# Order of the product blocks in seventeen of eighteen column-group pairs of a trunk kernel

## The chip, the cores and the metric

The kernel runs on one core of one Trainium2 chip. The metric is device time in microseconds, from the first to the last instruction of one execution; the median of the runs is compared. Lower is better.

## What is computed

The reference is a trunk of two layers on a sequence of 256 tokens with a model width of 2048: first a gated linear attention layer (GLA, 4 heads), then a retention layer (8 heads), each with an inner width of 4096, a silu gate, a norm in front and a residual add behind, and one last RMS norm.

```python
proj = h @ w_in                          # q, k, v, gate
q, k, v, gate = jnp.split(proj, ...)
...                                      # chunked attention with decay, per head
o = from_chunks(o)
o = o * lax.rsqrt(jnp.mean(o * o, axis=-1, keepdims=True) + EPS)   # GLA; retention: group norm
o = o.reshape(B, S, D_INNER) * head_g
return (o * jax.nn.silu(gate)) @ w_out
```

Nearly all of the arithmetic is in the products of the 256 tokens with the weights `w_in` and `w_out`.

## The kernel before

**Products.** Weights are read in groups of 512 columns; a group has 16 k-tiles of 128 rows. Float32 precision comes from three matmuls per k-tile and token tile: weights and activations are each split into a high part in a reduced format (hi) and the remainder (lo), and hi x xh, lo x xh and hi x xl are summed in PSUM (lines L360, L361 and L362 in pairs, L269 to L271 in single groups, L454 and L456 for q and k).

**Weights.** A raw chunk holds four k-tiles, 128 x 4 x 512, and is loaded by one DMA of 1 MB on SyncE's queue (L194) into one of four buffers (`raw`). A chunk is used as two units of two k-tiles. For each unit ScalarE writes hi (L220) and then VectorE lo = raw - hi (L221), two units ahead of TensorE, into three buffers each.

**Pairs.** Eighteen times, two groups of columns are computed together: a value group and a gate group of a head, or two groups of the output projection (then called first and second, too). For k-tiles 0 to 7 the two token tiles, two column groups and two halves of these k-tiles form a 2 x 2 by 2 x 2 block product, which is done with seven products (S1 to S7) where eight would be plain. Each S block is two units of six matmuls. K-tiles 8 to 15 are done plainly: V0 to V3 for the first group of columns and G0 to G3 for the second, one unit of twelve matmuls each. In the rows an `S4a` would be the first unit of S4, `S4b` the second.

**Combined weights.** Most of the seven products need sums of weight blocks. They are made in place in the raw chunk: when a unit of S1 has been split, GpSimd issues a DMA of 512 KB (L230) that adds another block of weights to it, and the result is what S5 needs; likewise S5 to S6, S6 to S4 (chunk x, of the first group) and S3 to S7 (chunk y, of the second). So S6 can be split only when the addend issued behind S5 has landed, S4 behind S6, S7 behind S3.

**Banks.** A pair has four result banks: "11" and "21" for the first column group (token tile 0 and 1), "12" and "22" for the second. S4 and V0 to V3 complete "21", S2 and V0 to V3 "11", S3 and G0 to G3 "12". The products S1, S6 and S7 go through one further bank (`psa`), S5 through another (`psb`), which becomes "22". When a bank is complete, VectorE adds it to its destination, the eviction: L737, L743 and L750 at the attention heads, L1023 at the output projection. The bank then goes to the next group.

**Order.** A tuple of block names per kind of pair is a hand-written order: `RET` for ten pairs next to attention heads (named g1p0, g2p0, g2p1, g3p0, and r0p, r1p, r2p, r4p, r5p, r6p for retention), `LATE` for two pairs of the output projection that open an output phase (ga0, gb0), `OUT` for five others (ga1, gb1, ra0, ra1, rb0), and `END` for the last pair (rb1). The same plan orders the loading of the chunks, the splits and the matmuls. ga0 and ga1, gb0 and gb1, ra0 and ra1, rb0 and rb1, and g2p0 and g2p1 follow each other without a group between them, which the text calls a join. Attention work, norms (L591 squares, L1027 multiplies by the norm's weights), rotary angles (L1216, L1217) and transposes run beside the products as side steps after each block. A scheduler places each engine's instructions, in the order given by priorities, so a side step may move by a few rows.

Of the kernel before, what the change touches and what calls it, by code (L numbers as in the profile page):

```python
# [57 lines left out]
def kernel(  # L58
# [60 lines left out]
        for j in range(raws_per_group):  # L119
            plan_units(plan_chunk(g, j))  # L120

    OUT = ("S1", "S2", "V0", "V1", "S5", "S3", "V2", "G0", "S6", "G1", "S7", "V3", "S4", "G2", "G3")
    RET = ("S1", "V0", "S2", "V1", "S5", "S3", "V2", "G0", "S6", "G1", "S7", "V3", "S4", "G2", "G3")

    LATE = ("S1", "S2", "V0", "V1", "S5", "S3", "G0", "G1", "S6", "V2", "S7", "V3", "S4", "G2", "G3")

    END = ("S1", "S2", "V0", "V1", "S5", "S3", "V2", "V3", "G0", "S6", "G1", "G2", "G3", "S7", "S4")

    def plan_pair(gp, gq, order):


        at = {}

        def chunk(key, g, j):
            if key not in at:
                at[key] = plan_chunk(g, j)
            return at[key]

        for block in order:
            kind, n = block[0], int(block[1])  # L140
            if kind in "VG":
                j, half = divmod(n, 2)
                c = chunk(kind + str(j), gp if kind == "V" else gq, 2 + j)
                units.append((c, half, half == 1, None))
            elif n == 2:
                plan_units(plan_chunk(gp, 1))
            else:
                c = chunk("y", gq, 1) if n in (3, 7) else chunk("x", gp, 0)
                plan_units(c, n in (4, 7), {1: (gq, 0), 5: (gq, 1), 6: (gp, 1), 3: (gq, 0)}.get(n))

    def plan_all():
        g = 0
        for part, (stage, heads) in enumerate((("gla", 2), ("gla", 2), ("ret", 4), ("ret", 4))):
            for h in range(heads * part, heads * part + heads):
                plan_group(g)
                if stage == "ret" and h % heads < heads - 1:
                    plan_pair(g + 1, g + 2, RET)
                    g += 3
                    continue
                if stage == "gla" and g > 0:  # L160
                    plan_pair(g + 1, g + 2, RET)
                    if h in TWICE:
                        plan_pair(g + 3, g + 4, RET)
                    else:
# [7 lines left out]
                g += rest + 1  # L172
            plan_pair(g, g + 1, LATE if stage == "gla" else OUT)
            plan_pair(g + 2, g + 3, END if g + 4 == n_groups else OUT)
            g += 4
# [726 lines left out]
    def gla_head(h):  # L902
# [37 lines left out]
        def gate_part():  # L940
            for t in range(2):
                silu(sgs[0], r, t)
                yield
# [32 lines left out]
        for gi in range(0 if h == 0 else 2 if h in TWICE else 1):  # L976
# [5 lines left out]
            if gi == 1:  # L982
                side.append(gate_part())
            pair_x(xhl, f"gp{g}_", "x0", pair_on(o, sg, v, r, r2, gi == 1, h in TWICE and gi == 0), RET, sparse=True)
            if cname:
# [45 lines left out]
    def out_half(first, final, name, later=None):  # L1031
# [13 lines left out]
        for pair in range(2):  # L1045
# [34 lines left out]

            order = END if last else LATE if pair == 0 and name[0] == "g" else OUT
            pair_x(ogt, f"{name}{pair}", name, on, order, drain_side, halves=last)
# [175 lines left out]
    def ret_head(h):  # L1258
# [86 lines left out]

        pair_x(xhl, f"rp{h}_", "x1", pair_on(o, sg, v, r, r2), RET)
        hw["sg"] = sg
# [124 lines left out]
```

## Time and profile before

| | |
|---|---|
| median of three runs | 1376.33 us (1376.2 to 1378.25) |
| profiled execution | 1376.41 us, of which the span is 1374.6 us |
| granted TensorE clock | 0.998 of full speed |
| TensorE matmul busy | 1359.6 us, 99% |
| TensorE weight load busy | 1133.4 us, 82% |
| VectorE busy | 1104.8 us, 80% |
| ScalarE busy | 832.0 us, 61% |
| GpSimd busy | 171.5 us, 12% |
| HBM read | 324.31 MB, mean 241 GB/s |

The profile covers one execution. Busy is the time in which an engine has an instruction running; matmuls overlap in the pipeline, so TensorE can be busy and still not at its full pitch. The span is shorter than the execution's time by what lies before the first and after the last instruction.

### The profile page before, as it was taken

The numbers are of one execution on the slowest core, as the hardware profiler recorded it, in microseconds if no ns is written. First come the engines' busy times: TensorE is split into PE (matmuls) and PEld (weight loads), VectorE is DVE, ScalarE is ACT, GpSimd is POOL, SyncE is SP. The second block draws the span as 40 slices with busy tenths as digits, with TensorE's granted clock in tenths as the row PEclk, the third lists the DMA queues.
The fourth block names the chain that finished last, engine by engine and source line by source line (L and its number), as shares of the span: only waits on it lengthen the run. The fifth ranks groups of instructions, "written<-read, shape, count | busy, mean of one in ns | idle before, by whom it ended". The sixth has DMA issues, their size and how long they took to land.

```text
span 1374.6 us, 17650 instructions
## 1 busy us (share of the span) xinstructions
PE 1359.6 (99%) x6500; PEld 1133.4 (82%) x6500; DVE 1104.8 (80%) x1517; ACT 832.0 (61%) x1060; POOL 171.5 (12%) x218
## 2 busy tenths in 40 slices
PE   8999999999999999999999999999999999999997
PEld 7888888888887888788888888888888888888876
DVE  6695896888897698887988888878768888887887
ACT  6676666655666766666655656446546465654665
POOL 1011110110122020111011111001201010100210
PEclk9999999999999999999999999999999999999999
DMA  9564785899899695699698969559989797964896
GB/s 359 212 245 161 208 252 188 208 273 317 233 267 275 179 266 197 189 262 281 184 296 262 292 204 291 180 191 254 266 341 236 251 236 252 241 246 165 226 299 170
DMA packets 58871, 331.76 MB, mean 241 GB/s; under 512 B 6928, under 2 KB 7440, under 8 KB 29856
## 3 DMA queue, kind: packets, MB, share of 16 engines
q1 hardware_dynamic: 34656, 238.96, 47.5%
q0 software_dynamic: 23408, 89.01, 32.7%
q10 hardware_dynamic: 720, 2.66, 0.5%
q8 instruction: 51, 0.84, 0.2%
q14 instruction: 36, 0.29, 0.1%
HBM read 324.31 MB, written 6.29 MB: 241 GB/s over the span
## 4 chain that ended last, share of the span: by engine, by line
PE 89%; DVE 4%; DMA 3%; ACT 2%; issue 1%; POOL 0%; ACTq 0%; DVEq 0%; POOLq 0%
PE rqk_ps L466 8%; PE rqk_ps L467 4%; PE rp__ps L361 4%; PE rp__ps L360 4%; PE rp__ps L362 4%; DMA raw<-in_w_all 3%; PE gqk_ps L466 2%; PE gv_ps L269 2%; PE gv_ps L270 2%; PE gv_ps L271 2%; DVE lo L221 2%; PE gg_ps L270 2%; PE gg_ps L269 2%; PE gp__ps L361 2%; PE gg_ps L271 2%; PE gp__ps L362 2%
## 5 line engine op out<-in xcount | busy, mean ns | idle before, releaser
L220 ACT ACTIVATE hi<-raw 128x1024 fp32r<-128x1024 f32 (+1 forms) x585 | 617.4, 1058 | 472.6 <-PE rqk_ps L466 69.0
L221 DVE TENSOR_TENSOR lo<-raw,hi 128x1024 fp32r<-128x1024 f32 (+1 forms) x585 | 710.4, 1223 | 228.2 <-ACT hi L220 221.2
L230 POOL DMA_DIRECT2D raw<-in_w_all x144 | 124.0, 861 | 653.7 <-DVE lo L221 450.9
L466 PE MATMUL rqk_ps<-xhl,hi 128*128 128x512 f32 x480 | 162.6, 397 | 0.0
L467 PE MATMUL rqk_ps<-xhl,lo 128*128 128x256 f32 x480 | 123.3, 281 | 0.0
L466 PEld LDWEIGHTS rqk_ps<-xhl,hi 128*128 128x128 f32 x480 | 88.1, 188 | 17.9
L467 PEld LDWEIGHTS rqk_ps<-xhl,lo 128*128 128x128 f32 x480 | 88.2, 189 | 3.6
L361 PE MATMUL rp__ps<-lo,xhl 128*128 128x512 f32 x192 | 74.9, 390 | 0.0
L362 PE MATMUL rp__ps<-hi,xhl 128*128 128x512 f32 x192 | 74.7, 389 | 0.0
L360 PE MATMUL rp__ps<-hi,xhl 128*128 128x512 f32 x192 | 69.8, 389 | 0.0
L361 PE MATMUL gp__ps<-lo,xhl 128*128 128x512 f32 x128 | 51.0, 399 | 0.8 <-DVE lo L221 0.8
L270 PE MATMUL gv_ps<-lo,xhl 128*128 128x512 f32 x128 | 50.9, 398 | 0.0
L270 PE MATMUL gg_ps<-lo,xhl 128*128 128x512 f32 x128 | 50.1, 392 | 0.0
L271 PE MATMUL gv_ps<-hi,xhl 128*128 128x512 f32 x128 | 50.0, 391 | 0.0
L362 PE MATMUL gp__ps<-hi,xhl 128*128 128x512 f32 x128 | 49.9, 390 | 0.0
L271 PE MATMUL gg_ps<-hi,xhl 128*128 128x512 f32 x128 | 49.9, 389 | 0.0
L466 PE MATMUL gqk_ps<-xhl,hi 128*128 128x512 f32 x144 | 49.4, 396 | 0.0
L360 PE MATMUL gp__ps<-hi,xhl 128*128 128x512 f32 x128 | 47.6, 393 | 0.3 <-ACT hi L220 0.3
L269 PE MATMUL gg_ps<-hi,xhl 128*128 128x512 f32 x128 | 46.7, 390 | 0.0
L269 PE MATMUL gv_ps<-hi,xhl 128*128 128x512 f32 x128 | 46.2, 393 | 0.0
L360 PEld LDWEIGHTS rp__ps<-hi,xhl 128*128 128x128 f32 x192 | 36.1, 188 | 7.5
L362 PEld LDWEIGHTS rp__ps<-hi,xhl 128*128 128x128 f32 x192 | 36.1, 188 | 7.5
(554 smaller groups left out, 2986.5 us busy)
## 6 DMA issues: line engine op xcount, KB each, us to landing
raw<-in_w_all SPq DMA_DIRECT2D x220, 1024.0 KB, 6.2
raw<-in_w_all POOLq DMA_DIRECT2D x144, 512.0 KB, 7.8
ogt<-xc POOLq DMA_DIRECT2D x2, 2048.0 KB, 11.8
resid<-in_x_n SPq DMA_DIRECT2D x2, 1024.0 KB, 13.0
xc<-ogt POOLq DMA_DIRECT2D x1, 2048.0 KB, 8.9
gg<-in_gn_g POOLq DMA_DIRECT2D x8, 256.0 KB, 4.0
gb<-in_gn_b POOLq DMA_DIRECT2D x8, 256.0 KB, 3.8
xc<-ogt ACTq DMA_DIRECT2D x1, 2048.0 KB, 7.5
```

What stands on the lines that cost most here:

```text
L220: a = nc.scalar.activation(hi[:, sl], src[:, sl], AF.Copy)
L221: b = nc.vector.tensor_tensor(lo[:, sl], src[:, sl], hi[:, sl].bitcast(F32), ALU.subtract)
L230: nc.gpsimd.dma_start(src, chunk_src(*then)[:, rows], accum_op=ALU.add)
L269: mm(ps, xh, hi[:, q, :], start=kt == 0, stop=False)
L270: mm(ps, xh, lo[:, q, :], start=False, stop=False)
L271: mm(ps, xl, hi[:, q, :], start=False, stop=kt == NKT - 1)
L360: mm(ps, xh, hi[:, q, :], start=start, stop=False, skip_group_check=True)
L361: mm(ps, xh, lo[:, q, :], start=False, stop=False, skip_group_check=True)
L362: mm(ps, xl, hi[:, q, :], start=False, stop=stop, skip_group_check=True)
L466: mm(ps[c], wh, rhs[:, kt, :, :], start=kt == 0, stop=False)
L467: mm(ps[c][:, 0, :], wl, rhs[:, kt, 0, :], start=False, stop=False)
```

## The change

The three tables `OUT`, `RET` and `LATE` change; `END` and all other code stay. S6 moves behind G1, that is behind both units that hold k-tiles 8 to 11 of the second group; S7 moves behind V3; S4 moves to the end of the pair.

```diff
--- before.py
+++ after.py
@@ -119,10 +119,10 @@
         for j in range(raws_per_group):
             plan_units(plan_chunk(g, j))
 
-    OUT = ("S1", "S2", "V0", "V1", "S5", "S3", "V2", "G0", "S6", "G1", "S7", "V3", "S4", "G2", "G3")
-    RET = ("S1", "V0", "S2", "V1", "S5", "S3", "V2", "G0", "S6", "G1", "S7", "V3", "S4", "G2", "G3")
-
-    LATE = ("S1", "S2", "V0", "V1", "S5", "S3", "G0", "G1", "S6", "V2", "S7", "V3", "S4", "G2", "G3")
+    OUT = ("S1", "S2", "V0", "V1", "S5", "S3", "V2", "G0", "G1", "S6", "V3", "S7", "G2", "G3", "S4")
+    RET = ("S1", "V0", "S2", "V1", "S5", "S3", "V2", "G0", "G1", "S6", "V3", "S7", "G2", "G3", "S4")
+
+    LATE = ("S1", "S2", "V0", "V1", "S5", "S3", "G0", "G1", "S6", "V2", "V3", "S7", "G2", "G3", "S4")
 
     END = ("S1", "S2", "V0", "V1", "S5", "S3", "V2", "V3", "G0", "S6", "G1", "G2", "G3", "S7", "S4")
```

The next rows are the order of instructions on an engine, without times. A number behind a name counts buffers; hi and lo are numbered by units through the whole program.

ScalarE at the end of the pair g2p1, before the change: hi177 is V3, hi178 and hi179 are S4, hi180 and hi181 G2 and G3; L713 is the silu of a gate, L734 and L495 belong to values.

```order
L220 ACTIVATE hi177_3714<-raw68_3490 128x1024
L220 ACTIVATE hi178_3724<-raw64_3248 128x1024
L734 ACTIVATE go5_3474<-gp5__psa_3477 128x512
L220 ACTIVATE hi179_3735<-raw64_3248 128x1024
L713 ACT_TABLE_LOAD
L713 ACTIVATE gsg4_3099<-gsg4_3099,rr_110 128x512
L220 ACTIVATE hi180_3759<-raw70_3610 128x1024
L495 ACTIVATE gv5_3476<-go5_3474,rr_110 128x512
L220 ACTIVATE hi181_3769<-raw70_3610 128x1024
```

The same place after the change: hi177 is the second unit of S7, hi178 and hi179 are G2 and G3, hi180 is the first unit of S4.

```order
L220 ACTIVATE hi177_3714<-raw67_3488 128x1024
L713 ACT_TABLE_LOAD
L713 ACTIVATE gsg4_3099<-gsg4_3099,rr_110 128x512
L220 ACTIVATE hi178_3738<-raw70_3610 128x1024
L495 ACTIVATE gv5_3486<-go5_3484,rr_110 128x512
L220 ACTIVATE hi179_3748<-raw70_3610 128x1024
L734 ACTIVATE go5_3484<-gp5__psa_3487 128x512
L220 ACTIVATE hi180_3759<-raw64_3248 128x1024
```

The load of the table and the silu stood between S4 and G2, and now stand between S7 and G2; the first split of S4 comes after both G blocks.

VectorE where ga1 ends and the q/k group g2qk begins, before: lo129 is G3, lo130 to lo132 are the first units of q/k; L1023 are evictions of the banks named ps21, ps12 and psb ("22").

```order
L221 TENSOR_TENSOR lo129_2849<-raw52_2691,hi129_2848 128x1024
L1023 TENSOR_TENSOR resid_104<-ga1_ps21_2616,resid_104 128x512
L1216 SCALAR_TENSOR_TENSOR ang_2583<-ang_2583 128x256
L221 TENSOR_TENSOR lo130_2862<-raw53_2703,hi130_2861 128x1024
L1217 TENSOR_SCALAR ang_2583<-ang_2583 128x256
L221 TENSOR_TENSOR lo131_2878<-raw53_2703,hi131_2877 128x1024
L1023 TENSOR_TENSOR resid_104<-ga1_ps12_2690,resid_104 128x512
L1023 TENSOR_TENSOR resid_104<-ga1_psb_2660,resid_104 128x512
L221 TENSOR_TENSOR lo132_2903<-raw54_2836,hi132_2902 128x1024
```

The same place after: lo128 and lo129 are S4, lo130 to lo132 again q/k.

```order
L221 TENSOR_TENSOR lo128_2839<-raw46_2421,hi128_2838 128x1024
L1217 TENSOR_SCALAR ang_2583<-ang_2583 128x256
L221 TENSOR_TENSOR lo129_2855<-raw46_2421,hi129_2854 128x1024
L1023 TENSOR_TENSOR resid_104<-ga1_ps12_2690,resid_104 128x512
L1023 TENSOR_TENSOR resid_104<-ga1_psb_2660,resid_104 128x512
L221 TENSOR_TENSOR lo130_2875<-raw53_2703,hi130_2874 128x1024
L221 TENSOR_TENSOR lo131_2885<-raw53_2703,hi131_2884 128x1024
L1023 TENSOR_TENSOR resid_104<-ga1_ps21_2616,resid_104 128x512
L221 TENSOR_TENSOR lo132_2903<-raw54_2814,hi132_2902 128x1024
```

The eviction of "21" stood ahead of the first q/k unit's lo and now stands behind the second unit's; those of "12" and "22" went the other way.

VectorE at the join of rb0 and rb1, before: lo565 is G3 of rb0, lo566 and lo567 are S1 of rb1, lo568 is the first unit of S2.

```order
L221 TENSOR_TENSOR lo565_11135<-raw214_10985,hi565_11134 128x1024
L1023 TENSOR_TENSOR resid_104<-rb0_ps21_10916,resid_104 128x512
L1027 TENSOR_TENSOR resid_104<-resid_104,fn0_10856 128x512
L221 TENSOR_TENSOR lo566_11152<-raw215_10997,hi566_11151 128x1024
L1027 TENSOR_TENSOR resid_104<-resid_104,fn0_10856 128x512
L221 TENSOR_TENSOR lo567_11169<-raw215_10997,hi567_11168 128x1024
L1023 TENSOR_TENSOR resid_104<-rb0_ps12_10984,resid_104 128x512
L1023 TENSOR_TENSOR resid_104<-rb0_psb_10958,resid_104 128x512
L221 TENSOR_TENSOR lo568_11201<-raw216_11122,hi568_11200 128x1024
```

After: lo565 is the second unit of S4 of rb0; lo566 to lo568 are the same units as above.

```order
L221 TENSOR_TENSOR lo565_11141<-raw208_10694,hi565_11140 128x1024
L1023 TENSOR_TENSOR resid_104<-rb0_ps12_10984,resid_104 128x512
L1023 TENSOR_TENSOR resid_104<-rb0_psb_10958,resid_104 128x512
L221 TENSOR_TENSOR lo566_11167<-raw215_10997,hi566_11166 128x1024
L1027 TENSOR_TENSOR resid_104<-resid_104,fn1_10858 128x512 x2
L1023 TENSOR_TENSOR resid_104<-rb0_ps21_10916,resid_104 128x512
L221 TENSOR_TENSOR lo567_11178<-raw215_10997,hi567_11177 128x1024
L221 TENSOR_TENSOR lo568_11201<-raw216_11100,hi568_11200 128x1024
```

Two L1027 and the eviction of "21" now stand between the two lo of S1, and nothing between the second of them and that of S2; before, one L1027 stood there, and two evictions behind it.

## Rows read from the trace of the kernel before

**Rows 1.** The page, part 1: busy us, share of the span, instructions.

```profile
PE 1359.6 (99%) x6500; PEld 1133.4 (82%) x6500; DVE 1104.8 (80%) x1517; ACT 832.0 (61%) x1060; POOL 171.5 (12%) x218
```

**Rows 2.** The chain that ended last, from 424 us: start, us, what.

```profile
425.05 10.03 DMA raw<-in_w_all
...
447.46 0.93 PE gqk_ps L454 x4
```

**Rows 3.** Busy time of each engine from 650 to 930 us.

```profile
650.00:930.00 280.00, 280.00 (x1389) 236.50 (x1387) 232.03 (x328) 158.73 (x194) 28.48 (x37) 1.00 0.78 239
```

**Rows 4.** Waits of TensorE in pairs: total us, times, longest.

```profile
PE gb_ps L361 <- DVE lo L221: 0.9, 3, 0.4
PE gp__ps L361 <- DVE lo L221: 0.8, 2, 0.5
PE ga_ps L361 <- DVE lo L221: 0.6, 2, 0.4
PE gp__ps L360 <- ACT hi L220: 0.3, 1, 0.3
...
PE rb_ps L361 <- DVE lo L221: 0.2, 1, 0.2
```

**Rows 5.** Timeline of TensorE, g2p1's end: start, us, what, [idle before].

```profile
437.53 0.50 PE L361 MATMUL gp__ps<-lo,xhl 128*128 128x512 f32 x1 [0.28 <-DVE lo L221]
437.87 0.39 PE L362 MATMUL gp__ps<-hi,xhl 128*128 128x512 f32 x1
...
439.26 0.50 PE L360 MATMUL gp__ps<-hi,xhl 128*128 128x512 f32 x1 [0.30 <-ACT hi L220]
...
440.52 0.51 PE L361 MATMUL gp__ps<-lo,xhl 128*128 128x512 f32 x1 [0.53 <-DVE lo L221]
```

**Rows 6.** The page, parts 5 and 6: groups of instructions, and DMA issues.

```profile
L221 DVE TENSOR_TENSOR lo<-raw,hi 128x1024 fp32r<-128x1024 f32 (+1 forms) x585 | 710.4, 1223 | 228.2 <-ACT hi L220 221.2
...
raw<-in_w_all POOLq DMA_DIRECT2D x144, 512.0 KB, 7.8
```

**Rows 7.** Timeline of ScalarE, the end of g2p1.

```profile
435.16 1.06 ACT L220 ACTIVATE hi<-raw 128x1024 fp32r<-128x1024 f32 x1 [2.25 <-DMA raw<-in_w_all]
436.24 1.28 ACT L713 ACT_TABLE_LOAD   x1
437.53 0.72 ACT L713 ACTIVATE gsg<-gsg,rr 128x512 f32<-128x512 f32 x1
```

**Rows 8.** Timelines of the weight loads and of VectorE, g2p1 to g3qk.

```profile
446.49 0.19 PEld L454 LDWEIGHTS gqk_ps<-xhl,hi 128*128 128x128 f32 x1 [0.42 <-DVE gsg L750]
...
445.75 0.68 DVE L750 TENSOR_TENSOR gsg<-gp__ps,gsg 128x512 f32<-128x512 f32 x1
```

**Rows 9.** Timelines of ScalarE and of TensorE at G2 of ga1.

```profile
326.52 2.01 ACT L220 ACTIVATE hi<-raw 128x1024 fp32r<-128x1024 f32 x2 [0.72 <-DMA raw<-in_w_all]
...
327.63 0.50 PE L360 MATMUL ga_ps<-hi,ogt 128*128 128x512 f32 x1 [0.25 <-ACT hi L220]
```

**Rows 10.** Timelines of VectorE, ScalarE and TensorE where rb0 meets rb1.

```profile
1326.93 0.68 DVE L1027 TENSOR_TENSOR resid<-resid,fn 128x512 f32<-128x512 f32 x1
1327.54 0.68 DVE L1061 TENSOR_TENSOR resid<-resid,rb_psa 128x512 f32<-128x512 f32 x1
...
1327.02 0.61 ACT L591 ACTIVATE sqj<-resid 128x512 f32<-128x512 f32 x1
...
1328.34 0.89 PE L360 MATMUL rb_ps<-hi,ogt 128*128 128x512 f32 x2
1329.40 0.50 PE L361 MATMUL rb_ps<-lo,ogt 128*128 128x512 f32 x1 [0.17 <-DVE lo L221]
...
1331.14 0.50 PE L361 MATMUL rb_ps<-lo,ogt 128*128 128x512 f32 x1
```

**Rows 11.** Timeline of VectorE behind the join of g2p0 and g2p1.

```profile
403.69 0.68 DVE L863 TENSOR_TENSOR w<-w,qk 128x256 f32<-128x256 f32 x1
...
407.24 0.28 DVE L861 TENSOR_TENSOR w<-lc 128x128 f32<-128x128 f32 x1
```

## The prediction, made before the changed kernel ran

> **What bounds the kernel now.** I read the page's busy times first: TensorE is busy for 1359.6 us, 99% of the span, VectorE for 80% and ScalarE for 61% [rows 1]. A full TensorE could still be slow inside, so I took its pitch next: four 512-column matmuls start within 0.93 us [rows 2], one per 0.23, and in the stretch from 650 to 930 us, which is retention pairs and q/k groups, it is busy for 280.00 of 280.00 [rows 3]. The change leaves every matmul in place, so it can only act on the moments at which TensorE waits. The view of waits lists them: in the pairs 0.9, 0.8, 0.6, 0.3 and 0.2 us of idle time [rows 4], and one of 0.25 at G2 of ga1 [rows 9]. A wait costs more than its idle time. A matmul shows 0.39 us although the next starts after 0.23, so 0.16 of the delay looks busy, and the first one after a wait shows 0.50, another 0.11 [rows 5]. I therefore price a wait at its idle time plus 0.27. With ten waits in all the pairs lose 3.1 + 2.7, about 6 us, some 0.4% of the span. Of these, the ones that open a pair behind a group stay as they are, since no block there moves.
>
> The reader should keep one cadence in mind. A unit of two k-tiles is split by ScalarE (hi, 1.06 [rows 7]) and then VectorE (lo, 1.22 [rows 6], or 1.14 from start to start when back to back, since the next one overlaps it by 0.08). TensorE works 12 x 0.227 = 2.72 on a V or G block and 6 x 0.227 = 1.36 on half of an S product. There are three hi and three lo buffers, so the hi of a unit can't start before TensorE has ended the unit three before it. A unit that stands behind two S units has 2.72 for 2.28 of splitting, and any further VectorE operation in front of its lo goes on TensorE's time.
>
> **What it removes.** (1) The fourth product's addend at the pair g2p1. The accumulating DMA issued at 425.05 took 10.03 us [rows 2]; ScalarE sat 2.25 for it, and a table load (1.28) and a silu (0.6 until the next starts) stood between this hi and that of G2 [rows 7]. TensorE waited 0.28 in S4b, then 0.30 and 0.53 in G2 [rows 5]: 1.11 + 3 x 0.27 = 1.9. After the change V3, S7, G2, G3 and S4a (12.2 us of TensorE) stand between S6b and S4b where G1, S7, V3 and S4a (9.5) stood, so the addend has 2.72 more than before, and it was only 0.28 + 0.16 late. The table load now stands ahead of the hi of G2. With t=0 at the end of V3, the hi of S7b ends by -1.6, the load by -0.3, the silu by 0.3, the hi of G2 by 1.4 and its lo by 2.6 to 2.8, against a first lo matmul at 2.72 + 2 x 0.227 = 3.17. So -1.9; its lower end is 0.9 left, if the lo comes 0.6 late.
>
> ScalarE's rows show the load ending at 437.52 and the silu starting at 437.53 [rows 7], with nothing between. The Trainium skill (ScalarE: Activation LUTs, section What ACT_TABLE_LOAD costs) gives the same 1.28 us for the load but adds a drain of 1.38 to every switch; the trace agrees with the first and shows no room for the second. By the page the lo of G2 would come at 4.2, and the sum below would be 1.0 + 0.3 higher here and 1.4 higher at the join of (5).
>
> (2) g2p1 to the next q/k group: its fourth bank waits 0.42 for L750, the eviction of "12" [rows 8], of which I count 0.27 as lost, since a weight load runs a little ahead of its matmul. "12" is now done a product earlier, and the bank that the fourth tile takes is that of "21", with six attention matmuls in front: -0.3. (3) G2 at ga1: its hi started on the raw chunk's landing [rows 9] and TensorE idled 0.25: 0.25 + 0.27 = -0.5. That chunk takes the buffer that G1's split frees, and G1 is now split right behind G0. Gains: 1.9 + 0.3 + 0.5 = **2.7**. In the nine other pairs of the RET order no wait of TensorE is released by a late split (the gp rows are g2p1's three, and there is no rp row [rows 4]), so more room for their addends is worth nothing.
>
> **What it adds.** S4 last means that the bank "21" is finished after "12" and "22", and that where two pairs meet six S units run on end (S4, S1, S2): each gives VectorE 1.36 us, and its lo takes 1.14. Three evictions (0.60 each from start to start, as L1027 [rows 10]) must fit in too.
>
> (4) ga1 to g2qk. The order shown has the eviction of "21" behind the lo of both first units of q/k. t=0 at the end of G3: eleven S4 matmuls remain (2.50), the fourth q/k matmul, which starts in that bank, is due at 2.50 + 3 x 0.227 = 3.17. The hi of g2qk/1 waits for S4a to leave its buffer (1.13) and ends at 2.25; its lo runs behind the previous one from 2.46 to 3.60; the eviction (0.68, as an L1027 or an L750 [rows 8, 10]) ends at 4.28. Late by 1.15 with the start-up, plus 0.11: **+1.25**. Bounds: 0, if the lo of g2qk/1 started before 1.3, and 1.7, if a hi is 0.4 later.
>
> (5) rb0 to rb1. t=0 as before; S4 ends at 2.72, S1a at 4.08. Before S1b's lo VectorE now has two evictions, the lo of S1a, two multiplications of L1027 and the eviction of "21". Evictions 0.06 to 1.3, lo S1a to 2.5; two L1027 (0.6 each from start to start [rows 10]) to 3.7, as the squares on ScalarE need only the two evictions (0.61 and an accumulator read, 0.72 each, to 2.5); eviction of "21" to 4.3; lo S1b to 5.5, where S1b's second matmul is due at 4.5: 1.0. The table load has moved between the hi of S1b and that of S2a, and V0, whose hi must wait for S1b and one more square, ends its lo at 10.5 against 9.7: 0.8. Three late points with 0.27 each give about 2.6, against 1.05 that this join loses today: L361 starts 1.06 behind the first of two L360 where two pitches, 0.45, would do (0.6), 0.11 behind it, and the same pattern of half the size in V0, whose L361 shows 0.50 [rows 10]. **+1.6**, bounds 0 (the join keeps its present loss) and +2.6.
>
> (6) g2p0 to g2p1. Between the lo of S4b and that of S1a VectorE now has two evictions (1.2), two products of w (0.68, so 0.6 from start to start) and four small ones (0.28, so 0.2) [rows 11]: from 0.3 on they last until 2.9, the lo of S1a until 4.1, and TensorE wants it at 3.2. **+1.1**, bounds 0 and 1.5. (7) gb0 to gb1: two squares, three evictions and transposes in the same six units; 1.05 against the present 0.4 + 0.27 [rows 4]: **+0.4**, bounds -0.65 and +1. (8) ga0 to ga1, ra0 to ra1 and the two v groups behind g1p0 and g3p0, where the last evictions stand just ahead of a lo with 0.0 to 0.3 in hand: together **+0.4**, bounds 0 and +2.
>
> Nothing else is priced: the number of DMAs, of splits and of evictions is the same, and SP's and GpSimd's issues move along with the units whose buffers they fill.
>
> **Sum**: -2.7 + 1.25 + 1.6 + 1.1 + 0.4 + 0.4 = **+2.0 us**. The profiled execution took 1376.41 us (1374.6 of span and 1.8 around it), and the median of the runs is 1376.33, so both give **1378.4**. A difference of 0.2% (2.75 us) is about the least that a measurement of this kernel can tell from no change.
>
> **Rivals.**
> *The joins hold (faster).* If VectorE enters each join a unit ahead, as it does today at most places, the evictions fit into that lead: then (4) to (8) cost 0 to 1 and 1373.6 to 1375 remains. For it: retention pairs run with no idle time at all at 80% VectorE [rows 1, 3]. Against it: the lead can be no more than the buffers allow, and my times above start from the earliest moment that they allow. The deciding point is the end of the lo of S1b at rb0|rb1, before or after 4.5 us behind G3. Chance 0.17; half of it passes -2.75.
>
> *The joins cost their upper bounds (slower).* One mechanism: VectorE has 8.2 us in six S units and a bill of 6 x 1.14 + 3 x 0.60 = 8.6, before any square, w or L1027; when its lead is gone before the run begins, each of these is paid in full. (4) 1.7, (5) 2.6, (6) 1.5, (7) 1.0 and (8) 2.0 are 8.8, less 2.7: +6, **1382.4**. For it: the DVE-released waits already outnumber the others [rows 4]. Against it: the long blocks G2 and G3 ahead of the run let VectorE catch up. It decides where the lo of S4b ends later than G3. Chance 0.25.
>
> *The addend was not the cause.* If S4's addend or G2's chunk lands as much later as it is wanted later, since the queues hold more at that moment (median 7.8 us today [rows 6]), the 2.4 of (1) and (3) stays and the additions come on top: +4.4, 1380.7. Against it: raw loads and addends keep their number and nearly their spacing. Chance 0.05.
>
> *A load of tables that blocks for longer.* If ScalarE is held for another 1.4 behind each of the two moved loads, G2 at g2p1 loses 1.3 of what (1) gives, and rb0|rb1 1.4 more: +4.7, 1381.1. The silu that follows a load within 0.01 us [rows 7] speaks against it. The Trainium skill (ScalarE: Activation LUTs, What ACT_TABLE_LOAD costs) is what would let one expect it. Chance 0.02.
>
> **How the numbers follow.** My sum has 0.51, with its own range from +0.3 to +3.3. Faster by more than 0.2%: half of the first rival, 0.08. Slower by more: 0.23 of the second rival, 0.06 of the last two and a tenth of the sum's own case, 0.05, which make 0.34. The rest, 0.58, is within 0.2%. The range that leaves out a tenth at each end runs from 1374.0, in the middle of the first rival, to 1382.0, just below the second's price.
>
> **What would show it.** Right: the three waits at g2p1 are gone and its ScalarE no longer waits for a DMA ahead of S4b; a wait of about 1 us in the L454 of the q/k group behind ga1, released by L1023; waits of L361 on lo at rb0|rb1 and g2p0|g2p1 of 0.5 to 1 us; no waits within the blocks of the retention pairs. Wrong: L454 starts at pitch there, or waits appear inside pairs at S6, V3 or S7, which I hold free.

## The result and the profile after

The changed kernel takes 1384.13 us (median of six runs, 1383.42 to 1387.11) against 1376.59 for the kernel before (six runs, 1376.2 to 1378.25). The ratio is 1.0056 with a 95% interval of 1.0046 to 1.0066, so it is slower by 6.3 to 9.1 us. The prediction was 1378.4 with a range up to 1382.0. The forecast was therefore wrong, by some 6 us and outside its range.

The page of the profiled execution after the change, its head and part 1 (answers to [rows 1]):

```profile
span 1381.6 us, 17654 instructions
...
PE 1361.2 (99%) x6500; PEld 1134.0 (82%) x6500; DVE 1106.9 (80%) x1517; ACT 831.3 (60%) x1060; POOL 173.0 (13%) x218
```

The span is 7.0 us longer, with the same 6500 matmuls, and TensorE's busy time grew by 1.6 only. The rest must be idle time, so the view of waits of TensorE comes next (total us, times, longest; answers to [rows 4]):

```profile
PE rqk_ps L466 <- DVE xhl L496: 2.4, 1, 2.4
...
PE rb_psa L361 <- DVE lo L221: 1.2, 1, 1.2
PE gqk_ps L454 <- DVE resid L1023: 1.0, 1, 1.0
PE gp__psa L361 <- DVE lo L221: 0.9, 1, 0.9
PE gb_ps L361 <- DVE lo L221: 0.8, 3, 0.4
...
PE gv_ps L270 <- DVE lo L221: 0.2, 1, 0.2
```

The first "..." stands for two waits of the opening, which are there before, too. Three of the first four rows shown are what the prediction named: the joins rb0|rb1 (term 5, `rb_psa`) and g2p0|g2p1 (term 6, `gp__psa`), and the fourth bank behind ga1 (term 4, `gqk_ps` released by the eviction L1023). The `gp__ps` rows of g2p1 are gone, as terms (1) and (3) wanted it. But the first row, the longest of all, is at a place that the prediction doesn't mention: the q/k group r0qk of the retention layer, which follows gb1.

The stretch that the prediction called full, 650 to 930 us (answer to [rows 3]; columns as there), starts with that wait. TensorE is busy for 2.41 us less than the 280.00 of before:

```profile
650.00:930.00 280.00, 277.59 (x1372) 234.46 (x1371) 230.81 (x323) 156.27 (x191) 27.79 (x36) 0.99 0.78 238
```

TensorE's timeline around it (start, us, instruction, [idle before]):

```profile
665.45 1.03 PE L694 MATMUL xt_tp<-ident,resid 128*128 128x128 f32 x8
668.89 0.79 PE L466 MATMUL rqk_ps<-xhl,hi 128*128 128x512 f32 x1 [2.41 <-DVE xhl L496]
...
669.70 0.63 PE L466 MATMUL rqk_ps<-xhl,hi 128*128 128x512 f32 x1
```

L694 transposes the residual (the layer's input) on TensorE, eight 128 x 128 blocks in a row; L496 on VectorE turns the transposed block into `xhl`, the hi and lo activations that L466 and L467 multiply. VectorE's timeline in the wait:

```profile
666.62 1.23 DVE L221 TENSOR_TENSOR lo<-raw,hi 128x1024 fp32r<-128x1024 f32 x1 [0.24 <-ACT hi L220]
667.76 0.68 DVE L307 TENSOR_TENSOR x_c<-x_f,x_c 128x512 f32<-128x512 f32 x1
668.36 0.48 DVE L496 SCALAR_TENSOR_TENSOR xhl<-xt_tp,smalls,xhl 128x256 fp32r<-128x256 f32 x1
```

The transposes are done at 666.5, but a lo (L221) and an addition of activation blocks (L307) stand ahead of L496 on VectorE, so the first `xhl` is ready at 668.84 and L466 starts at 668.89. VectorE isn't later here than before the change, when the same operations end at nearly the same times:

```profile
667.91 0.69 DVE L307 TENSOR_TENSOR x_c<-x_f,x_c 128x512 f32<-128x512 f32 x1
...
668.58 0.87 DVE L496 SCALAR_TENSOR_TENSOR xhl<-xt_tp,smalls,xhl 128x256 fp32r<-128x256 f32 x2
```

Before, TensorE goes on without a wait there: the `xhl` that VectorE writes at this time is one that is wanted later. The wait is 2.41, and it has a tail. Busy time in three stretches (us, then PE, PEld, DVE, ACT, POOL busy with counts, PEclk, DMA share, GB/s), after:

```profile
666.00:669.00 3.00, 0.59 (x6) 0.35 (x4) 2.76 (x7) 2.38 (x5) 0.00 (x0) 0.99 0.96 333
669.00:673.00 4.00, 4.00 (x14) 3.43 (x15) 3.49 (x13) 0.81 (x2) 0.00 (x0) 0.58 0.05 16
673.00:677.00 4.00, 4.00 (x25) 3.52 (x24) 2.36 (x2) 2.76 (x3) 0.00 (x0) 1.00 0.13 20
```

and the second of them before the change:

```profile
669.00:673.00 4.00, 4.00 (x24) 3.48 (x24) 4.00 (x8) 3.49 (x5) 0.00 (x0) 1.00 0.20 57
```

In the 4 us behind the wait the granted clock is 0.58, which means mostly the lower level of 1.2 GHz, and 14 matmuls fit in where 24 did: 10/24 x 4 = 1.7 us. Then it is 1.00 again. Wait and slow stretch make 4.1 us. In the prediction this place is free.

**Why these transposes.** The eviction of token tile 1 from a bank starts the transposes of its columns for the next layer. "21" of gb1 is column group 2, k-tiles 8 to 11 of the next layer; "22" is column group 3, k-tiles 12 to 15. Before, "21" was complete two blocks ahead of "22". TensorE's order there before (no times; `xt2_2` is group 2, `xt2_3` group 3, hi276 is r0qk's unit with k-tiles 8 and 9):

```
L694 MATMUL xt2_2_tp0_5527<-ident_103,resid_104 128x128 x3
...
L694 MATMUL xt2_3_tp1_5594<-ident_103,resid_104 128x128 x4
```

and after:

```
L694 MATMUL xt2_3_tp0_5542<-ident_103,resid_104 128x128 x3
...
L694 MATMUL xt2_2_tp1_5594<-ident_103,resid_104 128x128 x4
L466 MATMUL rqk0_ps0_5603<-xhl_107,hi276_5655 128x512
```

At the same place, directly ahead of hi276, stand the transposes of group 3 before, which are wanted two units later, and those of group 2 after, which the next matmul reads.

**The other places.** In the same profile, TensorE behind ga1 (answers to term 4) and at the join of rb0 and rb1 (answers to [rows 10]):

```profile
334.15 0.61 PE L454 MATMUL gqk_ps<-xhl,hi 128*128 128x512 f32 x2
335.80 0.50 PE L454 MATMUL gqk_ps<-xhl,hi 128*128 128x512 f32 x1 [1.03 <-DVE resid L1023]
...
1329.77 0.39 PE L360 MATMUL rb_psa<-hi,ogt 128*128 128x512 f32 x1
1331.40 0.50 PE L361 MATMUL rb_psa<-lo,ogt 128*128 128x512 f32 x1 [1.24 <-DVE lo L221]
```

Here L361 starts 1.63 behind L360 where a pitch is 0.23: 1.40, and five more delays of 0.1 to 0.8 behind it, up to V0, make 2.2 for this join, 1.15 more than it loses before (1.05). At ScalarE the load of the table at g2p1 stands where the prediction has it (answers to [rows 7]):

```profile
430.48 2.22 ACT L220 ACTIVATE hi<-raw 128x1024 fp32r<-128x1024 f32 x2
432.71 1.28 ACT L713 ACT_TABLE_LOAD   x1
434.01 0.72 ACT L713 ACTIVATE gsg<-gsg,rr 128x512 f32<-128x512 f32 x1
```

No idle time on a DMA is left there, and the silu starts 0.02 behind the load.

Summed over this one execution: r0qk +4.1, rb0|rb1 +1.15, ga1 +1.3, g2p0|g2p1 +1.2, the two v groups behind g1p0 and g3p0 together +0.5, the inside of rb1 +0.6, VectorE's last evictions another +0.9, and -2.7 from the three gains. That is +7.05, against +7.0 in the span. The match is closer than the list deserves: the opening, which no table touches, is 0.58 shorter in this execution (the third run of four L454 starts at 10.89, before at 11.47), so about as much must be lost in small delays that the list doesn't name.

### The profile page after: what moved, and what is told of

Read it like the earlier page. It is cut to its first block, busy times and chain, and to the rows that moved or that the text cites. A ratio compares the mean times of both kernels' runs of the same rounds, so it can differ in the third digit from the quotient of the medians.

```text
span 1381.6 us, 17654 instructions
## 1 busy us (share of the span) xinstructions
PE 1361.2 (99%) x6500; PEld 1134.0 (82%) x6500; DVE 1106.9 (80%) x1517; ACT 831.3 (60%) x1060; POOL 173.0 (13%) x218
## 4 chain that ended last, share of the span: by engine, by line
PE 92%; DVE 5%; ACT 1%; DMA 1%; issue 1%; ACTq 0%; DVEq 0%
PE rqk_ps L466 8%; PE rqk_ps L467 4%; PE rp__ps L361 4%; PE rp__ps L360 4%; PE rp__ps L362 4%; PE gqk_ps L466 2%; DVE lo L221 2%; PE gv_ps L270 2%; PE gp__ps L361 2%; PE gv_ps L271 2%; PE gp__ps L362 2%; PE gp__ps L360 2%; PE gv_ps L269 2%; PE gg_ps L270 2%; PE gg_ps L269 2%; PE gg_ps L271 2%
## 5 line engine op out<-in xcount | busy, mean ns | idle before, releaser
L221 DVE TENSOR_TENSOR lo<-raw,hi 128x1024 fp32r<-128x1024 f32 (+1 forms) x585 | 709.7, 1223 | 226.7 <-ACT hi L220 218.4
L230 POOL DMA_DIRECT2D raw<-in_w_all x144 | 124.1, 861 | 668.3 <-DVE lo L221 548.0
L466 PE MATMUL rqk_ps<-xhl,hi 128*128 128x512 f32 x480 | 163.3, 400 | 2.4 <-DVE xhl L496 2.4
L467 PE MATMUL rqk_ps<-xhl,lo 128*128 128x256 f32 x480 | 125.1, 283 | 0.0
L466 PEld LDWEIGHTS rqk_ps<-xhl,hi 128*128 128x128 f32 x480 | 89.2, 190 | 21.7 <-DVE xhl L496 2.7
L467 PEld LDWEIGHTS rqk_ps<-xhl,lo 128*128 128x128 f32 x480 | 89.1, 190 | 3.8
L361 PE MATMUL rp__ps<-lo,xhl 128*128 128x512 f32 x192 | 74.9, 390 | 0.0
L360 PE MATMUL rp__ps<-hi,xhl 128*128 128x512 f32 x192 | 69.9, 390 | 0.0
L361 PE MATMUL gp__ps<-lo,xhl 128*128 128x512 f32 x128 | 50.4, 394 | 0.0
L466 PE MATMUL gqk_ps<-xhl,hi 128*128 128x512 f32 x144 | 49.5, 396 | 0.0
L360 PE MATMUL gp__ps<-hi,xhl 128*128 128x512 f32 x128 | 47.6, 392 | 0.0
L360 PEld LDWEIGHTS rp__ps<-hi,xhl 128*128 128x128 f32 x192 | 36.1, 188 | 7.4
L361 PEld LDWEIGHTS rp__ps<-lo,xhl 128*128 128x128 f32 x192 | 36.1, 188 | 7.3
## 6 DMA issues: line engine op xcount, KB each, us to landing
resid<-in_x_n SPq DMA_DIRECT2D x2, 1024.0 KB, 11.4
xc<-ogt ACTq DMA_DIRECT2D x1, 2048.0 KB, 10.4
```

Source lines behind the costliest of these rows:

```text
L221: b = nc.vector.tensor_tensor(lo[:, sl], src[:, sl], hi[:, sl].bitcast(F32), ALU.subtract)
L230: nc.gpsimd.dma_start(src, chunk_src(*then)[:, rows], accum_op=ALU.add)
L360: mm(ps, xh, hi[:, q, :], start=start, stop=False, skip_group_check=True)
L361: mm(ps, xh, lo[:, q, :], start=False, stop=False, skip_group_check=True)
L466: mm(ps[c], wh, rhs[:, kt, :, :], start=kt == 0, stop=False)
L467: mm(ps[c][:, 0, :], wl, rhs[:, kt, 0, :], start=False, stop=False)
```

## The experiments

**The theories.** A: the +7.7 (the ratio times 1376.6) is mainly one wait, r0qk's for k-tiles 8 to 11, caused by the order in which gb1 finishes its banks; the joins cost about what the prediction has, and the gains are there. B: the joins and their VectorE bill cost more than one profile shows (the second rival), and r0qk's wait only takes up time that would be lost elsewhere. C: the gains that the profile shows aren't gains of the median, since g2p1's wait stood on the landing of one DMA in one execution.

The kernels below choose the table for each pair: the tables of before stay as `OUT0`, `RET0` and `LATE0`, and

```diff
+    NEW = ('gb1',)
+    pick = lambda n, a, b: a if n in NEW else b
...
-                    plan_pair(g + 1, g + 2, RET)
+                    plan_pair(g + 1, g + 2, pick(f"g{h}p0", RET, RET0))
```

and the same where the matmuls are written. `NEW` names the pairs that get the order of after, all others keep that of before. An experiment's edit is then its list `NEW` (all seventeen pairs where none is given), unless more is shown. Microseconds behind a ratio are its distance from 1 times 1376, with the interval's ends.

### r0qk's wait

**e1_swap**: the change, but gb1 computes its two column groups in exchanged roles, so that "21" is columns 3 and "22" columns 2. The work is the same.

```diff
-            plan_pair(g + 2, g + 3, ...)
+            plan_pair(g + 2 + (part == 1), g + 3 - (part == 1), ...)
...
-                    c = 2 * pair + n
+                    c = 2 * pair + (n ^ (name == "gb" and pair == 1))
```

> The changed kernel with the two column groups of gb1 exchanged, so that the eviction that now comes last belongs to the columns whose transposed k-tiles the next q/k group reads last. Theory: the wait of 2.4 us in the L466 behind gb1, and the slow matmuls behind it, are the order of the transposes alone; they go, 4.2 us less than the changed kernel, 1379.9. Rival: VectorE is simply late there, whichever columns come first; the wait stays within 1 us of its size, 1383 to 1384.

Measured: 1379.69 us, ratio to before 1.0023 [1.0014, 1.0032], +3.2 where the change has +7.7. The wait is gone; TensorE goes from the transposes into L466 at once, and the group that it reads was transposed 13 us earlier:

```profile
669.62 1.03 PE L694 MATMUL xt_tp<-ident,resid 128*128 128x128 f32 x8
670.41 0.48 PE L466 MATMUL rqk_ps<-xhl,hi 128*128 128x512 f32 x1
```

Some 4.5 us are this one wait and its tail (7.7 less 3.2, each uncertain by about 1.4). This is theory A's largest piece, if little more than half of the loss. The remaining +3.2 (1.9 to 4.4) is more than the +2.0 of the prediction, though its interval just reaches it. In its profiled execution (1381.92 us, 2.2 above its median) TensorE waits 0.34, 0.84, 0.76 and 0.92 inside ga1 at S5, where that of after doesn't wait; these come back below.

**e14_gb1**: the other direction, only gb1 in the new order (`NEW = ("gb1",)`, no exchange).

> The new order in gb1 alone, all other pairs as before. Theory: the wait of 2.4 us in the q/k group and the slow matmuls behind it appear as in the changed kernel, 4.2 less 0.5 for the shorter tail in front of it: 3.7 to 4.4 above before, 1380.4 to 1381.1. Rival: the wait needs gb0's new order too, within 1 of before.

Measured: 1379.75, ratio 1.0026 [1.0016, 1.0036], +3.6 (2.2 to 5.0). The wait is back, with the slow stretch behind it (granted clock 0.62 from 670 to 674 us, and 1.00 at this place in e1_swap), and nothing else of the change is in this kernel:

```profile
PE rqk_ps L466 <- DVE xhl L496: 2.4, 1, 2.4
```

So the cause is shown in both directions, by undoing it alone and by doing it alone. The two point at 4.5 and 3.6 us, the profile at 4.1.

### Which tables

**e2_ret** (`NEW` = the ten pairs of `RET`), **e3_out** (`NEW` = the seven pairs of `OUT` and `LATE`), **e4_g2p1** (`NEW = ("g2p1",)`), **e11_rb0** (`NEW = ("rb0",)`), **e12_ga0** (`NEW = ("ga0",)`).

> The new order in the ten RET pairs alone, OUT and LATE as before. Theory (places add up): -1.9 and -0.3 at g2p1, +1.2 at g2p0|g2p1, +0.5 at the v groups: -0.5 against before, 1376.1. Rival: the new order costs a little in every pair through later landings; ten pairs of seventeen would then give more than half of the loss, 1380 or more.

> The new order in the seven OUT and LATE pairs alone, RET as before. Theory (places add up): the changed kernel less what RET gives, +8.0 against before, 1384.6. Rival as for the run with RET alone: less than half of the loss, 1380 or less.

> The new order in the pair g2p1 alone, all other pairs as before. Theory: the waits of S4b and G2 (1.9) and of the fourth bank behind (0.3) go and nothing else moves, 1374.4. Rival: the addend was not the cause, or what it held up is late for another reason; 1376.0 to 1377.

> The new order in rb0 alone, all other pairs as before. Theory: the waits of the join grow from 1.05 to 2.2 us, the addends of S1 in the last pair land later for it, and VectorE carries a delay to the end: 1.2 to 2.6 above before, 1377.2 to 1378.6. Rival: the last pair makes up for it, within 0.5 of before.

> The new order in ga0 alone, all other pairs as before. There is no new wait at this join itself. Theory: S1 of ga1 is split 1.2 to 1.7 us later against TensorE, so its second addend lands late for S5 in many executions: a wait in psb and 12 at 300 to 312 us, 1 to 2.5 above before, 1377 to 1378.5. Rival: without the other pairs' changes the addend lands in time, 1375.5 to 1376.5.

| kernel | median us | ratio [95%] | us |
|---|---|---|---|
| e2_ret | 1377.14 | 1.0003 [0.9993, 1.0012] | +0.4 (-1.0 to 1.7) |
| e3_out | 1386.35 | 1.0067 [1.0051, 1.0083] | +9.2 (7.0 to 11.4) |
| e4_g2p1 | 1376.75 | 0.9996 [0.9987, 1.0005] | -0.6 (-1.8 to 0.7) |
| e11_rb0 | 1377.72 | 1.0007 [0.9995, 1.0018] | +1.0 (-0.7 to 2.5) |
| e12_ga0 | 1376.98 | 1.0006 [0.9992, 1.0019] | +0.8 (-1.1 to 2.6) |

As far as the intervals tell, the whole loss is in the output projection's tables. The ten `RET` pairs neither gain nor lose anything that can be told, although terms (1) and (2) gain 2.2 there and (6) and the v groups cost 1.6: about the sum of these.

e4_g2p1 speaks for theory C in part. The three waits at g2p1 are gone in its profile, as in that of after, and yet the median moved by less than the 1.9 of term (1); the interval's end lies just short of it. Its execution shows waits elsewhere, 0.76 at g3p0 and 0.47 at ga1's G2. And the old order doesn't always have the full wait. In six of the profiled executions g2p1 has the old order, and TensorE's idle time in S4 and G2 there is 1.11 us (before; [rows 5]), 1.24 (e15_joins), 0.53 (e11_rb0), 0.29 (e3_out), 0.21 (e12_ga0) and 0 (e14_gb1), 0.56 on average; in none of the eleven with the new order does TensorE wait there. So the wait is no accident of one execution, and the new order does remove it, but the 1.11 that the prediction took is twice its mean, and a gain of half of term (1) lies inside e4's interval.

**e8_sel**: `NEW` = g2p1, the six retention pairs and ra1, so the new order only where no other pair follows and no bank is wanted at once.

> The new order in eight pairs alone: g2p1, the six retention pairs and ra1, behind which nothing waits for the bank 21; the other pairs as before. Theory: no new wait, and the landing waits of those eight pairs are gone, 1375 to 1376. Rival: landings in these pairs were no loss on average, only in the profiled execution, 1376.5 to 1377.

Measured: 1375.72, ratio 1.0001 [0.9991, 1.001]. No loss, and no gain that can be told. In its profiled execution g2p1 waits for a landing, too, some 20 us ahead of the old place, on its ScalarE and then on TensorE:

```profile
417.95 2.00 ACT L220 ACTIVATE hi<-raw 128x1024 fp32r<-128x1024 f32 x2 [2.00 <-DMA raw<-in_w_all]
...
419.06 0.50 PE L360 MATMUL gp__ps<-hi,xhl 128*128 128x512 f32 x1 [1.06 <-ACT hi L220]
```

This wait isn't the new order's: e11_rb0 and e3_out, with the old order in g2p1, have 0.85 and 1.06 at the same place. With e4_g2p1 and e2_ret, e8_sel is the best of the new order's versions, and none of the three can be told from the kernel before.

### What is left without r0qk's wait

**e5_swap_rb0old**: e1_swap with rb0 in the old order (`NEW` without rb0). **e6_swap_evict**: e1_swap with the eviction of "21" at ga1 ahead of the lo of the second q/k unit, by the order of issue:

```diff
-            with behind_splits() if i >= len(units) - ENDS else nullcontext():
+            with behind_splits() if i >= len(units) - ENDS else tc.issue_after(latest[2]) if i == 131 else nullcontext():
...
-        look = LOOK if i < len(units) - 2 * ENDS else ENDS
+        look = LOOK - (i == 129) if i < len(units) - 2 * ENDS else ENDS
```

where `latest[2]` is that eviction's instruction.

> The kernel with gb1's groups exchanged, and in it the order of before for rb0 alone. Theory: the join rb0|rb1 costs not only its own waits (2.2 us against 1.05 before) but takes the lead of S1's lo, so the addends that this lo releases land late for S5, and the last chunk and the closing norm follow: 2.6 us less than with the exchange alone (1379.7), 1377.1. Rival: only the waits at the join itself count, 1.1 less, 1378.6.

> The kernel with gb1's groups exchanged, and in it the eviction of 21 at ga1 placed ahead of the lo of the second q/k unit on VectorE. Theory: the fourth matmul of the next q/k group waits 0.1 to 0.2 instead of 1.0, 1.1 us less than with the exchange alone (1379.7), 1378.6. Rival: the wait moves on to the lo behind the eviction, 1379.7.

Measured: 1379.21, ratio 1.0027 [1.0015, 1.0038] and 1379.51, ratio 1.0025 [1.0017, 1.0034]. Neither can be told from e1_swap's 1.0023, though the intervals are too wide to exclude 1 us. The edits did what they were for. In e6's profile the second L454 wait of 1.03 is gone, since the eviction stands between the two lo:

```profile
332.73 1.23 DVE L221 TENSOR_TENSOR lo<-raw,hi 128x1024 fp32r<-128x1024 f32 x1 [0.45 <-ACT hi L220]
334.07 0.69 DVE L1023 TENSOR_TENSOR resid<-ga_ps,resid 128x512 f32<-128x512 f32 x1
334.68 2.35 DVE L221 TENSOR_TENSOR lo<-raw,hi 128x1024 fp32r<-128x1024 f32 x2
```

and in e5's profile there is no `rb_psa` wait. But their medians don't show the 1 to 1.5 us each. What e5's profile does show, as e1_swap's does, is a group of waits that after's doesn't have, inside ga1 at S5: 0.31, 0.76 and 0.93. They begin on ScalarE:

```profile
304.18 2.95 ACT L220 ACTIVATE hi<-raw 128x1024 fp32r<-128x1024 f32 x3 [3.37 <-DMA raw<-in_w_all]
```

S5's second unit waits for the addend that was issued behind S1's second unit. So a new suspect is the S1 of a pair that follows another: with six S units on end, ScalarE and VectorE have no lead there, and S1's addends start late.

**e7_mid**: in the nine pairs with a join behind them or a bank that is wanted at once S4 stands ahead of G3 instead of behind it; g2p1, the retention pairs and ra1 as in after.

```diff
+    MID = ('g1p0', 'g2p0', 'g3p0', 'ga0', 'ga1', 'gb0', 'gb1', 'ra0', 'rb0')
+    pick = lambda n, a, b: a[:13] + ("S4", "G3") if n in MID else a if n in NEW else b
```

> The new order everywhere, but in the nine pairs that are followed by another pair, a v group or a q/k group with evictions on its path, S4 stands ahead of G3, so that 21 is finished before 12 and 22 as it was before the change. Theory: the structural waits (q/k behind gb1 2.4, rb0|rb1, g2p0|g2p1 and ga1) go; what is left is the room that the earlier G1 and the later S6 give to the landings, 1374.5 to 1376. Rival: S4's addend has no more room there than before the change and the landing waits remain, 1376.5 to 1377.5.

Measured: 1380.54, ratio 1.0036 [1.0023, 1.005]. r0qk's wait is gone, since "21" is finished ahead of "22" again, and so are those of L454 behind ga1 and of S1 at the joins. Still it is +5.0. Waits stand in S5 of ga1 (0.76 and 0.93, as in e5), ra1 (0.77) and gb1 (0.22), g2p1 has 0.56 behind its S1, and rb1 keeps 0.62 and 0.67 a few units behind the join.

**e15_joins**: `NEW = ("ga0", "gb0", "ra0")`, only the pairs ahead of a join whose second pair has S5's addend as its next need.

> The new order in ga0, gb0 and ra0 alone, whose joins show no wait of their own. Theory: S1 of the next pair is split 1.2 to 2 us later against TensorE, its second addend misses S5 in some executions, most at ga1: 0.5 to 2.5 above before, 1377.2 to 1379.2. Rival: the addends have room enough, within 0.5 of before.

Measured: 1380.04 (1375.01 to 1384.29), ratio 1.0021 [1.0008, 1.0035], +2.9 (1.1 to 4.8). In the profile, ga1 again:

```profile
305.55 0.50 PE L361 MATMUL ga_psb<-lo,c_d 128*128 128x512 f32 x1 [0.76 <-DVE lo L221]
308.14 0.50 PE L361 MATMUL ga_ps<-lo,c_d 128*128 128x512 f32 x1 [0.93 <-DVE lo L221]
```

The step before these is GpSimd's issues of S1's two addends (L230), before the change and in this kernel:

```profile
290.46 0.87 POOL L230 DMA_DIRECT2D raw<-in_w_all  x1 [16.05 <-DVE lo L221]
292.81 0.86 POOL L230 DMA_DIRECT2D raw<-in_w_all  x1 [1.48 <-DVE lo L221]
```

```profile
291.94 0.86 POOL L230 DMA_DIRECT2D raw<-in_w_all  x1 [18.63 <-DVE lo L221]
293.06 0.86 POOL L230 DMA_DIRECT2D raw<-in_w_all  x1 [0.26 <-DVE lo L221]
```

Before they are 2.35 apart, the first of them early. Now they are 1.12 apart, one issue right behind the other, as the lo of S1's two units end one behind the other. The second DMA is the one that S5b waits for, and how long it takes decides. In three executions with this pattern (after, e12_ga0, e5_swap_rb0old) the second issue is at 294.01, 293.88 and 293.79, and ScalarE's hi of S5b, released by the DMA each time, starts at 301.71, 301.51 and 304.18: 7.7, 7.6 and 10.4 us later. With the first two TensorE doesn't wait, with the third it does. The other executions agree. Eleven have S4 of ga0 moved. In six of them (after, e6, e9, e10, e12, e13) this DMA lands 7.1 to 8.0 us behind its issue, and TensorE doesn't wait at ga1's S5; in five (e1, e3, e5, e7, e15) it lands after 10.0 to 11.5, and TensorE waits. In the six with ga0 in the old order it lands after 7.1 to 8.9, with no wait. e12_ga0's row, a harmless case, with the same releaser:

```profile
301.51 1.06 ACT L220 ACTIVATE hi<-raw 128x1024 fp32r<-128x1024 f32 x1 [1.98 <-DMA raw<-in_w_all]
```

This fits the spread of e15's twelve runs, 9.3 us against 6.3 in the 28 of before beside them, and e12_ga0's profile without a wait there. What makes the same DMA take 7.6 us in one execution and 10.4 in the next was not found: the DMA engines are full in both kinds (share 1.05 between 296 and 300 us in after and in e5). The counts suggest that it is the two issues so close together; that is not shown.

### An attempt to mend S5, and its lesson

**e9_exchange**: e6_swap_evict with S3 ahead of S5 in ga1, gb1 and ra1, so that S5's addend gets a block more. **e10_fixall**: the same, with rb0, g2p0 and g1p0 in the old order.

```diff
+    EXC = ("ga1", "gb1", "ra1")
+    pick = lambda n, a, b: a[:4] + ("S3", "S5") + a[6:] if n in EXC else a if n in NEW else b
```

> The kernel with gb1's groups exchanged and ga1's eviction placed early, and in it S3 ahead of S5 in ga1, gb1 and ra1, so that S1's addends have one product more to land. Theory: what varies is the landing of S1's second addend for S5 behind a join, 0 to 3.9 us in the profiles so far; no wait is left in psb and 12 at the opening of ga1, and the time is 1 to 2.5 us less than without the exchange (1379.5), 1377 to 1378.5. Rival: the landings are not what is left, 1379 to 1380.

> The same kernel, and in it the order of before for rb0, g2p0 and g1p0 too, so that every cost named so far is removed while 14 of 17 pairs keep the new order. Theory: nothing else costs, 1375 to 1376.5, as before the change. Rival: the new order costs within its pairs too, 1378 or more.

Measured: 1384.93, ratio 1.0047 [1.003, 1.0064] and 1381.71, ratio 1.0034 [1.0021, 1.0048]: no better than e6, and e9 worse. S5's waits are gone in both profiles, as expected, though five of nine other executions with ga0's new order and S5 in its place have them and four don't, so two profiles say little. But S6 needs the addend that is issued behind S5, and S5 now stands a block later: V2, G0 and G1 (8.2 us of TensorE) instead of S3 and these (10.9) are left for it. e9's view of waits has them in the bank of S6:

```profile
PE ra_psa L361 <- DVE lo L221: 1.0, 2, 0.8
PE ga_psa L361 <- DVE lo L221: 0.8, 1, 0.8
PE gb_psa L361 <- DVE lo L221: 0.8, 1, 0.8
PE gb_psa L360 <- ACT hi L220: 0.7, 1, 0.7
```

They start at a landing. GpSimd's issue behind S5b at ga1, and ScalarE's hi of S6b:

```profile
309.21 0.86 POOL L230 DMA_DIRECT2D raw<-in_w_all  x1 [0.60 <-DVE lo L221]
...
319.13 2.96 ACT L220 ACTIVATE hi<-raw 128x1024 fp32r<-128x1024 f32 x3 [1.89 <-DMA raw<-in_w_all]
```

A wait has come up further along the chain of addends, at S6 in place of S5. The 8.2 us alone don't explain it: before the change S3, V2 and G0, also 8.2, lie between S5 and S6, and TensorE waits at no S6. What e9 has besides is the order of issue. GpSimd issues four addends within 7 us at this place, before the change those behind S5 first (301.56, 303.82) and those behind S3 next (306.77, 308.24), in e9 those behind S3 first (302.54, 304.80) and those behind S5 last (307.74, 309.21). Which of the two counts was not tested.

### All named causes but S5's landings taken out

**e13_named**: the new order in 14 pairs; gb1 exchanged (e1), ga1's eviction early (e6), and rb0, g2p0 and g1p0 in the old order. No exchange of S3 and S5.

> New order in 14 pairs, with gb1's groups exchanged and ga1's eviction placed early, and the order of before in rb0, g2p0 and g1p0; S5 stays where the change has it. Theory: all named waits are gone but the landings behind ga0, gb0 and ra0: 0.5 to 2 us above before, 1377.2 to 1378.7, and no wait of more than 0.6 outside psb and 12 of ga1. Rival: something unnamed costs, 1379 or more.

Measured: 1377.3 (1375.13 to 1383.11), ratio 1.001 [0.9997, 1.0022], +1.4 (-0.4 to 3.0). Of the 7.7 us some 6 go with the edits, give or take 2. What is left in its profile is S5 at ra1:

```profile
981.27 0.49 PE L360 MATMUL ra_psb<-hi,c_d 128*128 128x512 f32 x1 [0.79 <-ACT hi L220]
982.53 0.50 PE L361 MATMUL ra_psb<-lo,c_d 128*128 128x512 f32 x1 [0.77 <-DVE lo L221]
...
983.83 0.63 PE L362 MATMUL ra_psb<-hi,c_d 128*128 128x512 f32 x1
984.25 0.63 PE L360 MATMUL ra_ps<-hi,c_d 128*128 128x512 f32 x1
```

Behind these waits, too, a matmul takes 0.42 from start to start, about twice the pitch of 0.23, and the granted clock is low:

```profile
983.00:987.00 4.00, 4.00 (x13) 3.09 (x12) 3.56 (x4) 1.23 (x3) 2.35 (x3) 0.57 0.73 116
```

So S5's landings can cost more than their idle time. They don't always: behind e5's waits of 0.31, 0.76 and 0.93 the granted clock stays at 1.00.

## Why the prediction was wrong

**The step that failed: the sentence "Nothing else is priced", and term (7).** The sum has no term for gb1 and the q/k group behind it, r0qk. Term (7) has the "transposes in the same six units" at gb0|gb1 as a load on VectorE; it doesn't ask who reads them. The new order reverses the order in which "21" and "22" are finished, and I followed it only to the banks' next user (as in term 4). The evictions have a second reader, the transposes, and these a third, r0qk. In the sum this place stands at nothing. It costs 3.6 us by e14_gb1 (2.2 to 5.0), about 4.5 by e1_swap and 4.1 in the profile, more than any term of the sum. It could have been seen without a run: the order of TensorE after the change shows the transposes of group 2 directly ahead of the matmul that reads them.

**Terms (1) and (3), the gains: right in mechanism, too large for the median.** All three waits at g2p1, the bank behind it and G2 at ga1 disappeared as worked out, 2.7 us in one execution. But e4_g2p1 has -0.6 (-1.8 to 0.7) and e8_sel +0.1, so the 1.9 of (1) is not what the old order loses on average. In six executions of the old order the idle time there is 0 to 1.24 us, 0.56 on average, against the 1.11 that (1) started from. I subtracted a landing wait of one execution from the time of all; such a wait should have been a bound and not the value.

**Term (2)** can't be told apart, at 0.3. **Term (4) was right**: 1.03 idle, 1.3 with the start-up, for +1.25; the eviction stands where the order showed it, and with it moved (e6) the wait is gone, though the median didn't move measurably. **Term (6) came out right**: 0.94 idle, about 1.2 in all, for +1.1. Partly by luck, as its addition is 0.6 short: from 0.3 on, two evictions (1.2), two products of w (1.2) and four small operations (0.8) last until 3.5 and not 2.9, which would make the term 1.7. VectorE does spend 3.3 us there in the profile after (398.62 to 401.96). **Term (5) was right in its mechanism** and over-sized: +1.15 in the profile for +1.6, and e11_rb0 has +1.0 (-0.7 to 2.5).

**Term (7) at its own place** was over-sized: TensorE waits 0.27 us at gb0|gb1, before 0.38, for +0.4. **Term (8) was mis-sized in kind.** The v groups lose 0.5, inside what it has, and ga0|ga1 and ra0|ra1 show no wait at the join. The price there comes later, at S5: with six S units on end, S1's lo come as late as TensorE allows and their addends one right behind the other, so that S5 has little room, and none when the landing is a slow one. ga0, gb0 and ra0 together cost +2.9 (1.1 to 4.8, e15_joins) against 0.8 in terms (7) and (8). The prediction says that waits "inside pairs at S6, V3 or S7" would prove it wrong; it didn't think of S5. That this addend is what S5 waits for at ga1 is shown by the landings: 10.0 us or more in each of the five executions with the wait, 8.9 or less in each of the twelve without. Why the new order has slow ones in five of eleven executions and the old in none of six is not shown, and whether the mean cost is 1, 2 or 3 us is not settled, since e13_named, which also has these three pairs in the new order, has +1.4.

**The rivals.** The second, "the joins cost their upper bounds", names a time (1382.4) near the measured one, but not the cause: the joins cost what the sum has. Joins that hold: no. An addend as late as it is wanted late: not at S4, but at S5. The load of tables that blocks for longer: no, the silu follows within 0.02 us in both places. The Trainium skill (ScalarE: Activation LUTs, What ACT_TABLE_LOAD costs) has 1.28 us for the load, which the rows have too, and a drain of 1.38 besides, for which the trace has no room.

**The account.** The parts measured alone add up to 3.6 (gb1) + 2.9 (ga0, gb0, ra0) + 1.0 (rb0) + 0.4 (`RET`) + 1.3 (ga1, from the profile) = 9.2 for the measured 7.7, and each of the measured ones is uncertain by more than 1 us. So the largest part, r0qk, is shown by experiment; how the other 3 to 4 us divide among S5's landings, the joins and ga1 is in part argued.

## What to carry to other kernels

When a change moves the moment at which a result is finished, follow every reader of it to the first instruction of TensorE that needs it, not only the next user of its buffer: here the order of two evictions decided which transposed block came last, and the next group wanted just that one first. A wait for a DMA's landing that one profile shows is one draw; price it between nothing and its size, or by its mean over several executions. And where a product feeds a DMA that a later product waits for, moving the first one later, or its splits closer together, can be a cost at the later one.

## What the runs showed of the hardware

The clock: one wait of 2.41 us, with TensorE busy for 0.59 of 3 us, was followed by 4 us at a granted clock of 0.58 and then by 1.00 again, which added 1.7 us to it. Three waits of 0.35, 0.79 and 0.77 us within 7 us were followed by 4 us at 0.57 in e13_named, three of 0.31, 0.76 and 0.93 in e5_swap_rb0old by none below 1.00. The landing of one and the same accumulating DMA of 512 KB, issued within 0.3 us of the same moment in three executions, took 7.6, 7.5 and 10.3 us (after, e12_ga0, e5_swap_rb0old); over seventeen executions it took 7.1 to 8.9 us in twelve and 10.0 to 11.5 in five, with nothing in between.
